# Storing batches 4 and 5 by chosen DMA engines among the loads, and batch 11 in one transfer

## The chip, the cores and the metric

The kernel runs on one core of one Trainium2 chip. Times are device microseconds of one execution; lower is better. The kernel before takes 124.91 us (median of 3 runs, 124.83 to 125.43). The 16 DMA engines of the core are called by number, as the prediction does. The trace names none of them: a number stands for the share of the transfers that I planned for an engine. "SP's queue" and "ACT's queue" are the two that the page lists as hardware_dynamic (q1 with the stores, 18.70 MB, and q10 with the loads, 31.46 MB), "GpSimd's queue" the one that it lists as software_dynamic (q0, 0.18 MB). A run over 1.5% above the fastest of its kernel counts as slow. Each ratio is against the kernel before on the same chip and in the same rounds, so kernels are compared by their ratios and not by their times.

## The reference

```python
batch, m, k, n = 16, 512, 512, 512      # a: [16,512,512], b: [16,512,512], float32
return np.matmul(a, b.transpose(0, 2, 1)).astype(np.float32)
```

32 MB come in and 16 MB go out. The result is allowed to be computed in bf16 with float32 sums.

## The kernel before

Batches are worked on in eight pairs. Sixteen loads of 2 MB (even numbers from `a`, odd from `b`) are issued far ahead on ACT's queue (load 1 on SP's) into seven input buffers. DVE casts to bf16, PE transposes and multiplies, ACT copies the result from PSUM into one of seven output buffers (the eviction), and SP issues the stores. ACT must find output buffer `n % 7` free, so batch `n` waits for the store of batch `n - 7`. And the stores of SP's queue land in the order in which they were issued (batches 4 and 6 at 84.89 and 99.82 us).

```python
def landed(n):
    return s_st[n % NO], 16 * (n // NO + 1)          # NO = 7 output buffers
...
# ACT, pair u, half e
n = 2 * u + e
if n >= NO:
    nc.scalar.wait_ge(*landed(n - NO))
for j in range(J):
    nc.scalar.wait_ge(s_mm, J * n + j + 1)
    c = nc.scalar.copy(out=ob[:, n % NO, j, :]..., in_=ps[:, j, :]...)
...
# SP: batch X = 11 in pieces, every other batch in one transfer of 8 KB rows
store(n, lo=1, hi=J - 1)...                           # its middle rows, 128 partitions
store(n, step=J - 1, part=slice(32, 96))...
for i in range(4):
    store(n, step=J - 1, part=slice(i, 16, 4))...     # four partitions, planned for engines 0 to 3
store(n, step=J - 1, part=slice(16, 20))...           # engine 4's by plan, sent as four partitions
# GpSimd: the rest of batch 11, each time behind a dummy read of five rows
for i in range(4):
    nc.gpsimd.dma_start(turn[:5, i], a[0, :5, :64]...)
    for part in (slice(20 + i, 32, 4), slice(96 + i, P, 4)):
        store(X, step=J - 1, part=part, engine=nc.gpsimd)
```

The pieces of batch 11 are meant to take 16 KB off engine 4. The dummy reads are meant to move the next transfers on by five engines.

## Time and profile before

| | before |
|---|---|
| time | 124.91 us |
| span of the profiled execution | 123.3 us |
| DMA strip | full from slice 2 to 39 of 40 |
| last load lands | 99.78 us |
| last stores issued, landed | 114.33, 122.19 us |
| ACT's waits for a store | 1.50 us (batch 11), 4.42 us (batch 13) |

A strip has 40 equal slices; a digit is the busy share in tenths. The prediction shows the strips and ACT's waits, and how they are read. PE around the second to last pair: the second half of the transposes, then the 32 matmuls of the pair (columns: start, duration, engine, line, operation, out from in, count, and the idle time ahead).

```profile
88.82 1.05 PE L223 MATMUL tp<-ident,ha 128*128 128x128 bf16 x16 [0.68 <-PEq L135]
90.02 1.05 PE L223 MATMUL tp<-ident,hb 128*128 128x128 bf16 x16
90.91 7.29 PE L242 MATMUL ps<-tb,ta 128*128 128x512 bf16 x32
```

PE idles 0.68 us and then runs (90.9 to 98.2 us). The first matmuls of the last pair and the last copies of the run are:

```profile
105.55 7.29 PE L242 MATMUL ps<-tb,ta 128*128 128x512 bf16 x32
...
112.44 1.07 ACT L201 COPY ob<-ps 128x512 f32<-128x512 f32 x2 [0.60 <-PE ps L242]
```

The end of the run in stretches of 2 us (last two columns: DMA share and GB/s):

```profile
114.00:116.00 2.00, 0.00 (x0) 0.00 (x0) 0.00 (x0) 0.00 (x0) 0.00 (x0) 1.00 0.99 418
116.00:118.00 2.00, 0.00 (x0) 0.00 (x0) 0.00 (x0) 0.00 (x0) 0.00 (x0) 1.00 1.04 441
```

All compute is done, and the DMA engines work off the stores.

### The profile page before, as it was taken

The numbers are of one execution on the slowest core, as the hardware profiler recorded it, in microseconds if no ns is written. First come the engines' busy times: TensorE is split into PE (matmuls) and PEld (weight loads), VectorE is DVE, ScalarE is ACT, GpSimd is POOL, SyncE is SP. The second block draws the span as 40 slices with busy tenths as digits, with TensorE's granted clock in tenths as the row PEclk, the third lists the DMA queues.
The fourth block names the chain that finished last, engine by engine and source line by source line (L and its number), as shares of the span: only waits on it lengthen the run. The fifth ranks groups of instructions, "written<-read, shape, count | busy, mean of one in ns | idle before, by whom it ended". The sixth has DMA issues, their size and how long they took to land. (4 is left out here: it accounts for less than half of the span.)

```text
span 123.3 us, 2255 instructions
## 1 busy us (share of the span) xinstructions
PE 90.2 (73%) x768; PEld 54.8 (44%) x768; DVE 67.9 (55%) x96; ACT 67.9 (55%) x130; POOL 8.5 (7%) x18
## 2 busy tenths in 40 slices
PE   0000089999999899989998999999799917996000
PEld 0000078447744764574477347645654506542000
DVE  0000598982896589388918974872977059400000
ACT  0400064567855966696589468765866069656000
POOL 2000000000000000000000000000000039910000
PEclk9999999999999999999999999999999999999965
DMA  4999999999999999999999999999999999999991
GB/s 112 404 425 425 441 431 431 431 431 441 425 436 425 425 361 415 444 423 425 431 433 425 431 423 425 436 444 428 423 423 441 412 423 423 432 397 432 425 407 72
DMA packets 5341, 50.35 MB, mean 408 GB/s; under 512 B 904, under 2 KB 904, under 8 KB 1500
## 3 DMA queue, kind: packets, MB, share of 16 engines
q10 hardware_dynamic: 2160, 31.46, 60.5%
q1 hardware_dynamic: 2796, 18.70, 36.2%
q0 software_dynamic: 384, 0.18, 0.5%
q14 instruction: 1, 0.01, 0.0%
HBM read 33.56 MB, written 16.78 MB: 408 GB/s over the span
## 5 line engine op out<-in xcount | busy, mean ns | idle before, releaser
L242 PE MATMUL ps<-tb,ta 128*128 128x512 bf16 x256 | 57.8, 379 | 0.4
L201 ACT COPY ob<-ps 128x512 f32<-128x512 f32 x64 | 34.2, 591 | 27.8 <-PE ps L242 21.9
L181 ACT COPY ta<-tp 128x512 bf16<-128x512 bf16 x64 | 33.0, 612 | 13.7 <-PE tp L223 13.2
L242 PEld LDWEIGHTS ps<-tb,ta 128*128 128x128 bf16 x256 | 24.1, 98 | 30.6 <-issue 4.0
L223 PE MATMUL tp<-ident,ha 128*128 128x128 bf16 x256 | 18.6, 224 | 18.7 <-PEq L135 18.2
L223 PEld LDWEIGHTS tp<-ident,ha 128*128 128x128 bf16 x256 | 15.8, 100 | 22.3 <-issue 20.5
L168 DVE COPY tb<-tp 128x1024 bf16<-128x1024 bf16 x32 | 21.2, 685 | 3.6 <-DVEq L135 3.6
L223 PE MATMUL tp<-ident,hb 128*128 128x128 bf16 x256 | 17.6, 223 | 3.5 <-PEq L135 3.3
L223 PEld LDWEIGHTS tp<-ident,hb 128*128 128x128 bf16 x256 | 15.4, 100 | 4.7 <-issue 4.4
L154 DVE CAST ha<-ld 128x1024 bf16 x8 | 5.5, 690 | 14.6 <-POOLq L108 13.8
L163 DVE COPY ha<-wa 128x2048 bf16<-128x2048 bf16 x8 | 5.5, 691 | 12.7 <-DVEq L135 12.7
L154 DVE CAST hb<-ld 128x1024 bf16 x8 | 5.5, 689 | 7.9 <-DVEq L135 7.9
L158 DVE CAST wa<-ld 128x2048 bf16 x8 | 9.8, 1220 | 0.0
L158 DVE CAST wb<-ld 128x2048 bf16 x8 | 9.8, 1220 | 0.0
L114 POOL DMA_DIRECT2D turn<-in_a_dram x4 | 2.7, 663 | 98.9 <-ACT ob L201 98.9
L155 DVE CAST ha<-ld 128x1024 bf16 x8 | 5.5, 687 | 0.0
L155 DVE CAST hb<-ld 128x1024 bf16 x8 | 5.5, 686 | 0.0
L167 DVE COPY hb<-wb 128x2048 bf16<-128x2048 bf16 x8 | 5.5, 684 | 0.0
L98 POOL DMA_DIRECT2D out_dram<-ob x8 | 5.2, 651 | 0.0
L176 ACT ACT_TABLE_LOAD x1 | 1.3, 1283 | 4.1 <-issue 4.1
L78 POOL TENSOR_SCALAR_AFFINE_SELECT ident<-ident 128x128 bf16<-128x128 bf16 x1 | 0.3, 288 | 0.2 <-POOL ident L76 0.2
L76 POOL MEMSET ident<- 128x128 bf16 x1 | 0.2, 205 | 0.5 <-SPq L41 0.5
(5 smaller groups left out, 0.6 us busy)
## 6 DMA issues: line engine op xcount, KB each, us to landing
ld<-in_a_dram ACTq DMA_DIRECT2D x8, 2048.0 KB, 29.1
ld<-in_b_dram ACTq DMA_DIRECT2D x7, 2048.0 KB, 26.8
out_dram<-ob SPq DMA_DIRECT2D x14, 1024.0 KB, 29.0
ld<-in_b_dram SPq DMA_DIRECT2D x1, 2048.0 KB, 12.5
out_dram<-ob SPq DMA_DIRECT2D x1, 768.0 KB, 8.0
out_dram<-ob SPq DMA_DIRECT2D x1, 512.0 KB, 24.5
out_dram<-ob SPq DMA_DIRECT2D x2, 256.0 KB, 7.9
out_dram<-ob POOLq DMA_DIRECT2D x4, 32.0 KB, 6.0
```

The lines of the kernel that those rows point to most:

```text
L98: return engine.dma_start(out[n].rearrange("(p j) n -> p j n", j=J)[part, rows], ob[part, n % NO, rows])
L114: nc.gpsimd.dma_start(turn[:5, i], a[0, :5, :64].rearrange("p (x k) -> p x k", x=2)[:, :, :16]).then_inc(s_y, 16)
L154: nc.vector.tensor_copy(out=h[:, :J, :], in_=src[:, :J, :HK])
L155: nc.vector.tensor_copy(out=h[:, J:, :], in_=src[:, J:, :HK]).then_inc(s_c, 1)
L158: nc.vector.tensor_copy(out=w[:], in_=src[:, :, HK:]).then_inc(s_w, 1)
L163: nc.vector.tensor_copy(out=ha[:], in_=wa[:]).then_inc(s_ca, 1)
L167: nc.vector.tensor_copy(out=hb[:], in_=wb[:]).then_inc(s_cb, 1)
L168: nc.vector.tensor_copy(out=tb[:, ko, :], in_=tp[:, 2 + ko % 2].rearrange("k j p -> k (j p)"),).then_inc(s_eb, 1)
L181: c = nc.scalar.copy(out=ta[:, ko, e * J * P:(e + 1) * J * P].rearrange("k (j p h) -> k j p h", j=J, h=2), in_=tp[:, ko % 2, :, e * HP:(e ...
L201: c = nc.scalar.copy(out=ob[:, n % NO, j, :].rearrange("m (p j) -> m p j", j=2 * J), in_=ps[:, j, :].rearrange("m (j p) -> m p j", j=2 * J),)
L223: t = nc.tensor.transpose(tp[:, 2 * x + g, j, :], h[:, j, g * P:(g + 1) * P], ident[:])
L242: t = nc.tensor.matmul(ps[:, j, :], ta[:, ko, (e * J + j) * P:(e * J + j + 1) * P], tb[:, ko, :].rearrange("k (j p) -> k j p", j=2 * J)[:, ...
```

## The change

The intent: move the piecewise stores from batch 11, near the end, to batches 4 and 5, among the loads; send full 8 KB rows; and take 32 KB off engine 4 in place of 16.

```diff
-    X = 11
+    X = 4
...
+        def store_two(part, engine):                      # both batches, 8 KB per row and batch
+            return engine.dma_start(
+                out[X:X + 2].rearrange("e (p j) n -> p e (j n)", j=J)[part],
+                ob[part, X % NO:X % NO + 2].rearrange("p e j n -> p e (j n)"))
+        def spare(i):                                      # on GpSimd's queue
+            last = [slice(96 + i, P, 4)]
+            if i < 2:
+                nc.gpsimd.dma_start(turn[:5, i], ...)      # dummy read of five rows
+                parts = [slice(20 + i, 32, 4)]
+            elif i == 2:
+                parts = [slice(16, 17), slice(17, 18), slice(16 + i, 32, 4)]
+            else:
+                parts = [slice(i, 32, 4)]
+            for part in parts + last:
+                store_two(part, nc.gpsimd).then_inc(s_y, 16)
+            # called for i = 0, 1 after load 9 and for i = 2, 3 after load 10
...
-            # SP: batch 11 in seven transfers (cut)
+            # SP
+            if n == X + 1:
+                for part in (slice(32, 96), *(slice(i, 16, 4) for i in range(3))):
+                    store_two(part, nc.sync).then_inc(s_x, 16)
...
+                if n == X + NO:                            # ACT, batch 11
+                    nc.scalar.wait_ge(s_x, 16 * 4)
+                    nc.scalar.wait_ge(s_y, 16 * 12)
-                if n >= NO:
+                elif n >= NO and n != X + 1 + NO:
                     nc.scalar.wait_ge(*landed(n - NO))
```

Batch 11 now waits for both batches 4 and 5, and batch 12 for nothing.

More of the change, by code (lines that the diff above doesn't have):

```diff
@@ L93, in landed, with store @@
         def landed(n):
-            return s_st[n % NO], 16 * (n // NO + 1)
-        def store(n, lo=0, hi=J, step=1, part=slice(0, P), engine=nc.sync):
-            rows = slice(lo, hi, step)
+            return s_st[n % NO], 16 * (n // NO + (n % NO not in (X, X + 1)))
+        def store(n, lo=0, hi=J):
+            return nc.sync.dma_start(
+                out[n].rearrange("(p j) n -> p j n", j=J)[:, lo:hi], ob[:, n % NO, lo:hi]
+            )
+        def store_two(part, engine):
             return engine.dma_start(
-                out[n].rearrange("(p j) n -> p j n", j=J)[part, rows], ob[part, n % NO, rows]
+                out[X:X + 2].rearrange("e (p j) n -> p e (j n)", j=J)[part],
+                ob[part, X % NO:X % NO + 2].rearrange("p e j n -> p e (j n)"),
             )
@@ L105 @@
             load(n, nc.scalar)
+        def spare(i):
+            last = [slice(96 + i, P, 4)]
+            if i < 2:
+                nc.gpsimd.dma_start(
+                    turn[:5, i], a[0, :5, :64].rearrange("p (x k) -> p x k", x=2)[:, :, :16]
+                ).then_inc(s_y, 16)
+                parts = [slice(20 + i, 32, 4)]
[5 more added lines that the diff above has]
+                store_two(part, nc.gpsimd).then_inc(s_y, 16)
         for n in range(2 * pairs):
             nc.gpsimd.wait_ge(s_ld[n % NL], 16 * (n // NL + 1)).then_inc(s_go, 1)
-        nc.gpsimd.wait_ge(s_out, X + 1)
-        for i in range(4):
-            nc.gpsimd.dma_start(
-                turn[:5, i], a[0, :5, :64].rearrange("p (x k) -> p x k", x=2)[:, :, :16]
-            ).then_inc(s_y, 16)
-            for part in (slice(20 + i, 32, 4), slice(96 + i, P, 4)):
-                store(X, step=J - 1, part=part, engine=nc.gpsimd).then_inc(s_y, 16)
+            if n in (X + 5, X + 6):
+                nc.gpsimd.wait_ge(s_out, X + 2)
+                for i in range(2):
+                    spare(2 * (n - X - 5) + i)
         nc.sync.wait_ge(s_ld[0], 32)
@@ L122 @@
             nc.sync.wait_ge(s_out, n + 1)
-            if n != X:
+            if n == X + 1:
+                for part in (slice(32, 96), *(slice(i, 16, 4) for i in range(3))):
+                    store_two(part, nc.sync).then_inc(s_x, 16)
+            elif n != X:
                 store(n, hi=J if n < batch - 1 else J - 1).then_inc(landed(n)[0], 16)
-                continue
-            store(n, lo=1, hi=J - 1).then_inc(landed(n)[0], 16)
-            store(n, step=J - 1, part=slice(32, 96)).then_inc(s_x, 16)
-            for i in range(4):
-                store(n, step=J - 1, part=slice(i, 16, 4)).then_inc(s_x, 16)
-            store(n, step=J - 1, part=slice(16, 20)).then_inc(s_x, 16)
         def taker(engine):
@@ L256 @@
     with tc.tile_critical(sync_engine=act, no_gpsimd_drain=True):
-        nc.scalar.wait_ge(s_x, 16 * 6)
-        nc.scalar.wait_ge(s_y, 16 * 12)
         for n in range(batch - NO, batch):
```

## The prediction

> **What bounds the kernel now.** I read the strips of busy tenths first, then the DMA queues, the chain that ended last, the waits, and last the trace's list of packets and of semaphore updates (one update per DMA engine and transfer), which shows each engine's own end.
>
> ```profile
> PE   0000089999999899989998999999799917996000
> PEclk9999999999999999999999999999999999999965
> DMA  4999999999999999999999999999999999999991
> GB/s 112 404 425 425 441 431 431 431 431 441 425 436 425 425 361 415 444 423 425 431 433 425 431 423 425 436 444 428 423 423 441 412 423 423 432 397 432 425 407 72
> ...
> HBM read 33.56 MB, written 16.78 MB: 408 GB/s over the span
> ```
>
> The 16 DMA engines are full from the second slice to the last but one, at 397 to 444 GB/s but for one slice of 361, while PE is idle for the last 10 us. The kernel is a fixed 50.35 MB pushed through a full pipe: only less work on the pipe, or a more even end of its 16 engines, can shorten it. Two phases:
>
> ```profile
> core 0: us, PE busy (x) PEld busy (x) DVE busy (x) ACT busy (x) POOL busy (x), PEclk, DMA share, GB/s
> ...
> 53.00:99.00 46.00, 43.77 (x379) 26.22 (x376) 31.51 (x45) 30.46 (x59) 0.00 (x0) 1.00 1.01 428
> ...
> 105.00:114.00 9.00, 7.78 (x45) 3.50 (x42) 1.29 (x2) 5.45 (x11) 3.39 (x7) 1.00 1.03 416
> ```
>
> Until 99.8 us loads and stores share the pipe; after that stores alone, and while GpSimd's small transfers run the rate is 416 rather than 428. The chain that ended last is useless here as a bound: it gives 5.4% of the span to PE and 0.9% to the last evictions, and ends at 113.5 us, before the last stores. What it leaves out is the queue of stores behind it: the last 256 KB are issued at 114.33 us and land at 122.19.
>
> The waits matter because the change moves one of them:
>
> ```profile
> ACT ob L201 <- PE ps L242: 21.9, 28, 1.2
> ACT ta L181 <- PE tp L223: 13.2, 4, 10.8
> ACT ob L201 <- DMA out_dram<-ob: 5.9, 2, 4.4
> ```
>
> ```profile
> 84.91 2.05 ACT L201 COPY ob<-ps 128x512 f32<-128x512 f32 x4 [1.50 <-DMA out_dram<-ob]
> ...
> 99.84 2.05 ACT L201 COPY ob<-ps 128x512 f32<-128x512 f32 x4 [4.42 <-DMA out_dram<-ob]
> ```
>
> The 1.50 is batch 11 waiting for the store of batch 4 (same output buffer of seven; landed at 84.89), the 4.42 is batch 13 waiting for batch 6 (99.82).
>
> The packet list gives unit costs: a 16 KB packet takes 611 ns of one engine, 8 KB 309, 4 KB 159, 2 KB 84. The semaphore updates give the laggard. Fifteen engines have signalled batch 10's store by 109.22 us, the sixteenth at 110.35: 1.13 us late. After batch 11, which takes 16 KB off one engine, the lag is 0.56 (batch 12: 114.27 and 114.83), and 0.58 on the very last transfer (121.61 and 122.19). In the packet list the pipe empties between 120.4 and 121.1 us, except one engine that runs alone to 121.7.
>
> [...] the spare semaphore of batch 11 has 16 + 5 x 4 updates by engines plus 5 early ones, as one 16-engine and five 4-engine transfers would give. [...] between 53 and 99 us 2 MB of loads (16 KB packets) land per 7.33 us beside 1 MB of stores (8 KB packets). [...]
>
> **The change, part by part.**
>
> 1. Engine 4's share. Of batches 4 and 5 each engine normally writes 8 partitions x 2 x 8 KB = 128 KB. [...] after the change engines 0 to 3 write 136 KB, engine 4 96 KB, the rest 128. Before, in batch 11, engine 4 gave up 4 x 4 KB = 16 KB and engines 0 to 3 took 4 KB each. Net: engine 4 does 16 KB less, two packets x 309 ns = 0.62 us; engines 0 to 3 do 4 KB more, 0.15 us. If engine 4 is the laggard, it trails by only 0.58 us, so the end moves to the second-latest engine: 122.19 - 121.61 = 0.58 us at most, 0.43 if one of engines 0 to 3 is that second one.
> 2. Batch 11's rows. Today: 128 packets of 4 KB x 159, 168 of 2 KB x 84, 44 of 4 KB by GpSimd x 159 = 41.5 us of packet time; as 128 x 309 it is 39.6. The 1.9 us over 16 engines is 0.12 us. Two of four dummy reads go too (nothing). From the fill of the window 105 to 114 (416 against 428: 0.25 us over 9 us) the gain may be up to 0.25. I take 0.15.
> 3. Timing of loads. GpSimd's share of batches 4 and 5 is 832 KB: 64 KB on each of engines 5 to 15, 32 on engine 4, 24 on 0 to 3. It is issued after loads 9 and 10 have landed (55.9 and 63.2 us) and so comes as a third queue in the mixed phase, where before there were two. The loads behind it shift by 64 KB = 8 x 309 ns = 2.4 us on engines 5 to 15. The last load, 99.78 today, lands at about 102.0. Before to after the last load the work is fixed: 99.78 to the first matmul of the last pair at 105.55 is 5.77, so that pair starts at about 107.8 and ends about 2.3 us late.
> 4. Batch 11's wait. Its buffer is now free only when batches 4 and 5 are both out. On engines 0 to 3 the SP queue must finish 4 x 64 + 112 = 368 KB, where batch 5 before was the 384th KB, out at 90.1 to 91. 16 KB less is 1.8 us less at 7.33 us per 64 KB; 24 KB from GpSimd is 0.9 more: about 89.8, with stragglers 90.5. So the 1.50 us wait that ended at 84.91 ends about 90.5, though the data is ready about 2.4 us later too. The 4.42 us wait for batch 6 goes, since that store now lands by about 97.5 and batch 13 is not ready until 101. From 90.5: four copies 2.05, then `ta` 2.1, second half of the transposes and matmuls from about 96; 7.3 of matmul, and 4.9 from there to the next pair's first matmul (as 86.02 to 90.91 today): 108.2. It ties with the loads' 107.8.
> 5. Does the later compute reach the end? The last stores are issued 2.5 us later: batch 14 at 111.38 + 2.5 = 113.9, the last at 116.8. A load issued at 0.92 had its first packet at 1.96, so data flows 1.04 us after issue: 114.9. With 2 MB left at 2.46 us per MB and the pipe empty at about 120.6, batch 14 is needed at 115.6. The slack of today (3.2 us) shrinks to 0.7, but is not used up.
>
> Sum: 0.5 (part 1) + 0.15 (part 2), parts 3 to 5 hidden: 124.91 - 0.65 = 124.26. I take 124.3.
>
> **Rivals.** (a) The late compute starves the pipe at 115 us. Against it: 0.7 us of slack; for it: each microsecond that batch 11's wait ends after 90.5 comes off that slack, and then off the end. If the wait ends at 92.5, the kernel comes to about 125.5. (b) The laggard is not engine 4 but, say, one of engines 0 to 3, which get more: then the end would be later by 0.15, some 125.0. Against it: the lag halved from 1.13 to 0.56 just across batch 11, and 16 KB is 0.6 us. (c) GpSimd's issues, 0.56 to 1.14 us each today, sit in the loop that tells DVE of landed loads; six of them take 3.5 to 6 us, less than the 7.3 between loads, and the pair they could delay waits for batch 11's buffer anyway. No effect. (d) More gain: the pipe in the store phase runs at 428 throughout; then 123.7.
>
> **Range and chances.** Gains are capped by the second-latest engine (0.58) and the packet time; losses by the starved pipe, of which I give 20%, worth up to 1 us or more. 8 in 10: 123.7 to 125.2. A change over 2% needs 2.5 us: 2% for faster, as nothing that large is on the pipe, and 4% for slower.
>
> **What would show it.** Right: the last transfer's sixteenth update within 0.2 us of the fifteenth; GpSimd's queue at 0.85 MB; the last load landing about 2 us later; one wait of `ob` for a store, ending near 90.5; DMA strip full to slice 39. Wrong: a slice below 9 near 115 us in the DMA strip, or two waits for stores; the lag unchanged at 0.6, which would mean the wrong engine was relieved.

## The result, and the profile after

The changed kernel takes 126.95 us (126.74 to 127.12, 6 runs) against 125.08 us for the kernel before in the same rounds: ratio 1.0148, 95% interval 1.0127 to 1.0168. A ratio here is the mean time of one kernel's fast runs over that of the other's of the same rounds, so it is not quite the ratio of the medians. The change loses 1.5%, clearly outside the range predicted.

The strips of the changed kernel:

```profile
PE   0000189999999899989999998998304999999900
PEclk9999999999999999999999999999955589999995
DMA  3999999999999999999999999999999999999393
GB/s 105 435 435 424 424 429 435 435 445 424 419 424 424 429 364 432 448 398 432 435 416 430 414 443 419 435 424 424 445 411 437 427 416 429 416 424 388 152 422 123
```

The third digit from the end of the DMA strip is a hole: 152 GB/s in a slice of 3.1 us. PE has a gap at slices 29 to 31, half its clock (digit 5) in slices 30 to 32, and is then busy until two slices from the end, where before it was three. The same two stretches of the end:

```profile
114.00:116.00 2.00, 2.00 (x11) 0.89 (x10) 0.00 (x0) 1.23 (x3) 0.00 (x0) 1.00 0.77 324
116.00:118.00 2.00, 2.00 (x11) 0.88 (x9) 0.00 (x0) 1.07 (x2) 0.00 (x0) 1.00 0.12 49
```

PE and ACT are still at work while the DMA engines have run dry. At 428 GB/s these two stretches lose 2 x (1 - 324/428) + 2 x (1 - 49/428) = 2.3 us of transfer. Going back from there, ACT's waits and its copies of batch 11:

```profile
ACT ob L217 <- DMA out_dram<-ob: 9.0, 1, 9.0
...
92.35 2.05 ACT L217 COPY ob<-ps 128x512 f32<-128x512 f32 x4 [9.00 <-DMA out_dram<-ob]
...
118.21 1.07 ACT L217 COPY ob<-ps 128x512 f32<-128x512 f32 x2 [0.60 <-PE ps L258]
```

There is one wait in place of two, and it ends at 92.35 us. The last copies begin at 118.21 where before they began at 112.44. And PE in the pair behind that wait:

```profile
95.53 1.99 PE L239 MATMUL tp<-ident,ha 128*128 128x128 bf16 x16 [5.53 <-PEq L148]
97.31 1.91 PE L239 MATMUL tp<-ident,hb 128*128 128x128 bf16 x16
99.02 8.12 PE L258 MATMUL ps<-tb,ta 128*128 128x512 bf16 x32
...
111.32 7.29 PE L258 MATMUL ps<-tb,ta 128*128 128x512 bf16 x32
```

After 5.53 us of idleness the transposes take 1.99 and 1.91 us where they took 1.05, and the matmuls 8.12 where they took 7.29: the granted clock was 0.50 from 90.88 to 101.12 us. The last transfer's 16 updates come between 123.89 and 124.13 us. The laggard seems gone, but this proves nothing: an engine that was behind may have caught up while the others stood idle in the hole.

### The profile page after: what moved, and what is told of

The parts are those of the page before. It is cut to its first block, busy times and chain, and to the rows that moved or that the text cites.

```text
span 125.2 us, 2250 instructions
## 1 busy us (share of the span) xinstructions
PE 92.5 (74%) x768; PEld 56.6 (45%) x768; DVE 68.2 (54%) x96; ACT 68.0 (54%) x130; POOL 8.4 (7%) x18
## 5 line engine op out<-in xcount | busy, mean ns | idle before, releaser
L258 PE MATMUL ps<-tb,ta 128*128 128x512 bf16 x256 | 58.7, 384 | 0.4
L239 PE MATMUL tp<-ident,ha 128*128 128x128 bf16 x256 | 19.6, 230 | 23.0 <-PEq L148 22.5
L239 PEld LDWEIGHTS tp<-ident,ha 128*128 128x128 bf16 x256 | 16.5, 102 | 26.9 <-issue 25.1
L239 PE MATMUL tp<-ident,hb 128*128 128x128 bf16 x256 | 18.5, 230 | 2.7 <-PEq L148 2.7
L239 PEld LDWEIGHTS tp<-ident,hb 128*128 128x128 bf16 x256 | 16.3, 103 | 3.5 <-issue 3.2
L103 POOL DMA_DIRECT2D out_dram<-ob x10 | 5.9, 595 | 3.1 <-ACT ob L217 3.1
L120 POOL DMA_DIRECT2D turn<-in_a_dram x2 | 1.9, 926 | 54.8 <-DMA ld<-in_b_dram 54.8
## 6 DMA issues: line engine op xcount, KB each, us to landing
ld<-in_b_dram SPq DMA_DIRECT2D x1, 2048.0 KB, 12.3
```

Source lines behind the costliest of these rows:

```text
L103: return engine.dma_start(out[X:X + 2].rearrange("e (p j) n -> p e (j n)", j=J)[part], ob[part, X % NO:X % NO + 2].rearrange("p e j n -> p ...
L120: nc.gpsimd.dma_start(turn[:5, i], a[0, :5, :64].rearrange("p (x k) -> p x k", x=2)[:, :, :16]).then_inc(s_y, 16)
L239: t = nc.tensor.transpose(tp[:, 2 * x + g, j, :], h[:, j, g * P:(g + 1) * P], ident[:])
L258: t = nc.tensor.matmul(ps[:, j, :], ta[:, ko, (e * J + j) * P:(e * J + j + 1) * P], tb[:, ko, :].rearrange("k (j p) -> k j p", j=2 * J)[:, ...
```

## The experiments

Thirteen kernels ran, and all gave correct results. Theory A is the late release of batch 11's buffer and what follows from it. Theory B is that GpSimd's transfers among the loads cost the time as such, C that batch 11 in one transfer does. D and E came up on the way.

**1. The wait alone.** The kernel before, with no transfer changed:

```diff
-                    nc.scalar.wait_ge(*landed(n - NO))
+                    nc.scalar.wait_ge(*landed(n - NO + (n == 11)))
```

> The kernel before, with one wait changed: batch 11's eviction waits for the store of batch 5 (lands near 92.4 us) in place of batch 4 (84.9). No transfer is changed. Theory A (the late release of batch 11's buffer and what follows of it on PE empties the store queue): the last pair's copies end near 118 to 119 us in place of 113.5, the DMA strip has a hole of 2 to 3 us near 116, time 127.3 to 127.8, ratio 1.018 to 1.022 (the hole, without the change's gain). Theory B (GpSimd's transfers among the loads and the later last load cost the time): 125.1, ratio 1.000. Theory C (batch 11 in one transfer costs it): 125.1.

Measured: 125.92 us (125.29 to 126.69), ratio 1.0090 (1.0050 to 1.0130). The wait ends at 91.51, the last copies begin at 116.90, and the strip has the hole:

```profile
DMA  4999999999999999999999999999999999999793
GB/s 122 408 423 423 434 429 423 445 434 439 434 423 429 429 352 431 439 405 431 421 426 455 421 421 434 413 439 431 429 429 431 416 421 431 412 412 424 304 416 124
```

So the wait by itself makes a loss of 0.9%, with no transfer touched, against B and C. The size was missed by half: the wait ended 0.8 us sooner than in the changed kernel, the last copies came 1.3 us sooner, and from 114 to 118 us some 0.9 us of transfer are lost (356 and 311 GB/s) against 2.3.

**2. The transfers without the wait.** An eighth output buffer was not tried. The input buffer of load 9 has been read by 62 us and is never filled again, so batches 11 and 12 can be evicted into it:

```diff
+        def obuf(n):
+            if n in (11, 12):
+                return ld[:, 2, (n - 11) * J:(n - 10) * J, :]
+            return ob[:, n % NO]
...
-                if n == X + NO:  ...wait for s_x and s_y
+                if n >= NO and n not in (11, 12):
```

> The changed kernel, with batches 11 and 12 evicted into an input buffer that is no longer used, so that nothing waits for batches 4 and 5; all transfers stay. Theory A: no wait for a store at batch 11, no hole in the DMA strip, last transfer's 16 updates within 0.25 us, time 124.2 to 124.6, ratio 0.993 to 0.996. Theory B: still 126.5 to 127, ratio 1.013, with the last load still landing near 102. Theory C: the same 127.

Measured: 125.35 us (125.21 to 125.44), ratio 1.0033 (1.0013 to 1.0054).

```profile
DMA  5999999999999999999999999999999999999991
GB/s 143 398 430 424 430 430 430 430 430 430 424 430 435 424 382 390 448 419 440 409 424 433 422 430 432 422 414 427 427 451 424 435 406 430 424 422 424 424 411 42
```

The hole is gone, and with it 1.0148 - 1.0033 = 1.15%, or 1.4 us. That is theory A. But the kernel is still slower than before, not 0.5% faster: the other half of my expectation failed. The last transfer's updates say where: eleven engines finish by 121.21 us, three at 121.4 to 121.5, one at 122.07 and one at 122.42. Something other than engine 4's old lag holds the end.

**3. The wait where it can be made up.** Batches 2 and 3 in place of 4 and 5, so that batch 9 waits:

```diff
-    X = 4
+    X = 2
```

> The changed kernel with batches 2 and 3 in place of 4 and 5, so that the buffer that comes free late is wanted by batches 9 and 10, two pairs before the end's last three. Theory A: a wait of 3 to 6 us at batch 9 that ends near 76.5 us, made up again because a pair takes 11.5 us of PE but 14.6 us of loads; no hole at 116, time 124.2 to 124.7, ratio 0.993 to 0.997. Theory B (the transfers themselves): 127.

Measured: 125.36 us (125.32 to 125.69), ratio 1.0041 (1.0019 to 1.0063), with no hole and this wait:

```profile
77.89 2.05 ACT L217 COPY ob<-ps 128x512 f32<-128x512 f32 x4 [6.09 <-DMA out_dram<-ob]
```

Again the hole is cured and the gain does not come. Its updates end as in experiment 2: two engines at 122.18 and 122.40, the rest by 121.64.

**What the packets say (theory D).** The trace lists every packet with start, duration and size but not its engine. Yet on a full engine the next packet starts 3 or 4 ns before the one before ends, so packets can be chained into 16 engines, and each engine's role read from its own sequence on GpSimd's queue (a dummy read shows 128 bytes, a row 8 KB). Checked on the kernel without any special transfer (experiment 4), the chains give every engine the 3,072 KB that it must have (one of them 8 KB more, a packet of the kind that the page lists as instruction). For experiment 2 they give:

```
engines (by their part in GpSimd's transfers)   KB in all       last packet ends, us
0, 1 (got both one-row transfers)               3104, 3112      121.74, 122.10
2, 3                                            3088            121.18, 121.19
4                                               3040            120.58
5 to 11                                         3072            120.49 to 120.95
12 to 15                                        3056            120.21 to 120.60
planned: 0 to 3 3080, 4 3040, the rest 3072
```

(One engine's 8 KB of instructions are in the 3112.) The two one-row transfers, rows 16 and 17, went to the same two engines, and what follows went four engines lower than planned. (The expectations below call the place at which GpSimd's next transfer starts the cursor.) Two engines carry 32 KB more than most, 4 x 309 ns = 1.2 us: that is the late end. Engine 4 was relieved as planned. In the kernel before, the chains confirm it as the laggard: it ends at 121.73, the rest by 121.16, although it has 16 KB less; its packets took 3.1 us longer than the standard duration of their sizes, those of the other engines 1.1 to 1.6.

**4. No chosen engines at all.** The kernel before with batch 11 as an ordinary store, and nothing on GpSimd's queue:

```diff
-            if n != X:
-                store(n, hi=J if n < batch - 1 else J - 1).then_inc(landed(n)[0], 16)
-                continue
-            # the seven transfers of batch 11, and GpSimd's twelve (cut)
+            store(n, hi=J if n < batch - 1 else J - 1).then_inc(landed(n)[0], 16)
```

> The kernel before without any transfer by chosen engines: each batch goes in one transfer (the last one in two). It says what 16 KB off one engine and the 2 KB rows of batch 11 are worth. My reading of the laggard: the last transfer's sixteenth update comes 1.1 us after the fifteenth (0.58 in before), the other engines end 0.15 us earlier; time 125.4 to 125.6, ratio 1.003 to 1.005. If the special transfers of batch 11 were a loss in themselves: below 125.0.

Measured: 125.26 us (124.94 to 125.67), ratio 1.0030 (1.0006 to 1.0055). The sixteenth update comes at 122.03, the fifteenth at 121.39: 0.64 us apart, not 1.1. The direction was right, and the other engines do end 0.2 us earlier than before (121.39 against 121.61). By the ratios, relieving engine 4 by 16 KB was worth about 0.3% (interval 0.06 to 0.55), net of the small rows that it took. The two profiles are weaker evidence, as the lag itself differs between executions: at batch 6, before any relief, the sixteenth update was 0.22 us late here and 0.87 in the kernel before.

**5. Repair of the placing, first try.** Experiment 2 with a dummy read of two rows after each one-row transfer:

```diff
             for k, part in enumerate(parts + last):
                 store_two(part, nc.gpsimd).then_inc(s_y, 16)
+                if i == 2 and k < 2:
+                    nc.gpsimd.dma_start(turn[:2, 2 + k], a[0, :2, :64]...).then_inc(s_y, 16)
```

> The kernel with freed buffers (125.35 us), plus two dummy reads of two rows on GpSimd's queue, one after each of the two one-row transfers. Chaining the packets of that run by their end times puts both one-row transfers on the same two DMA engines, and everything after them four engines too low: two engines write 32 KB more than the rest in all and end 1.2 us late, where the plan was 8 KB on each of four. Theory D (this misplacing eats the gain): the dummies put each row on its own pair; four engines have 8 KB more, the last transfer's sixteenth update falls from 122.4 to about 121.4, time 124.2 to 124.5, ratio 0.994 to 0.997. If the second row stays on the first pair in spite of the dummy: 124.5 to 124.8. Rival (GpSimd's transfers among the loads cost as such, misplaced or not): 125.3 as without the dummies.

Measured: 124.83 us (124.66 to 125.04), ratio 0.9976 (0.9957 to 0.9995), the first one below 1. The last update is at 122.00, not 121.4. The chains show the second case that I had written down: the dummies moved what follows to the right engines, but both rows still went to engines 0 and 1 (3,088 KB), with 2 and 3 at 3,072. 16 KB of excess are gone from each of two engines, and 0.57% of the time with them.

**6. Does a small packet cost a turn (theory E)?** The changed kernel, with SP's three four-row transfers each cut in two; same bytes, same engines:

```diff
-                for part in (slice(32, 96), *(slice(i, 16, 4) for i in range(3))):
-                    store_two(part, nc.sync).then_inc(s_x, 16)
+                store_two(slice(32, 96), nc.sync).then_inc(s_x, 16)
+                for i in range(3):
+                    for e in range(2):
+                        store(X + e, part=slice(i, 16, 4)).then_inc(s_x, 16)
```

> The changed kernel with each of the three four-row transfers on SP's queue cut into two, one per batch: the same bytes on the same engines, three more semaphore packets on each of engines 0 to 3. Theory E (a semaphore packet takes a turn like any packet, in which another queue's 16 KB packet of 0.61 us passes): batch 11's wait ends about 1.8 us later, near 94.2 in place of 92.35; the hole grows, time 128.3 to 129. Rival (bytes alone set when the buffer comes free): 92.4, time 126.9.

Measured: 128.42 us (127.09 to 129.29, 4 runs, the highest of them slow), ratio of the fast runs 1.0214 (1.0162 to 1.0267). The wait of batch 11:

```profile
93.89 2.05 ACT L219 COPY ob<-ps 128x512 f32<-128x512 f32 x4 [10.43 <-DMA out_dram<-ob]
```

It ends 1.54 us later with not a byte more: three semaphore packets on each of four engines cost 0.51 us each, near the 0.61 us of the load packet that passes in the meantime. The semaphore updates of the changed kernel agree: its three small transfers end on the last of engines 0 to 3 at 87.63, 89.89 and 92.33 us, 2.3 and 2.4 us apart, where two 8 KB packets take 1.83 at 7.33 us per 64 KB. In the chains a load packet stands behind each of these semaphore packets. The kernel before shows the same turns from 53 to 99 us: of 798 load packets of 16 KB, 797 are followed on their engine by a packet of SP's queue; of 808 store packets of 8 KB, 788 are followed by a packet of the loads' queue; and of 111 semaphore packets of SP's queue all are, 105 of them by one of 16 KB. The time follows the wait by the ratio, 1.0214 against 1.0148, though the two intervals touch: two fast runs took 128.33 and 128.51 us, as expected, and one 127.09.

**7. No relief of engine 4, but the rest of the change.** All of rows 0 to 31 by GpSimd in eight-row transfers, no one-row transfer, no extra transfers on SP's queue:

```diff
-                for part in (slice(32, 96), *(slice(i, 16, 4) for i in range(3))):
+                for part in (slice(32, 96),):
...
-            if i < 2:      # dummy and parts as planned
-            elif i == 2:
+            # for every i: parts = [slice(i, 32, 4)], no dummy
```

> The changed kernel without any relief of engine 4: rows 0 to 31 all go by GpSimd's queue in eight transfers of eight rows, rows 32 to 95 by SP's, no one-row transfer, no dummy read, every engine 128 KB. Theory A and D: SP's queue ends the pair near 86.5 us, so batch 11 waits 2 to 3 us and no hole opens; engine 4 is the only late one again (sixteenth update 0.6 us after the fifteenth); time 125.0 to 125.4, ratio 1.001 to 1.005. Theory B (any storing by GpSimd among the loads costs): 126 or more.

Measured: 125.48 us (125.19 to 125.86), ratio 1.0039 (1.0018 to 1.0059). There is no hole, the sixteenth update is 0.87 us after the fifteenth, and the wait is short:

```profile
86.53 2.05 ACT L217 COPY ob<-ps 128x512 f32<-128x512 f32 x4 [3.42 <-DMA out_dram<-ob]
```

Without the extra transfers on SP's queue (48 KB and three semaphore packets on each of engines 0 to 3) the buffer comes free 5.8 us sooner. GpSimd's storing among the loads costs nothing by itself that these runs resolve (0.39% with full lag, where experiment 4 without it has 0.30%), against B once more.

**8. Control.** The kernel before with the freed input buffer of experiment 2 (its `obuf`, and no wait at 11 and 12).

> Control: the kernel before with batches 11 and 12 evicted into the same unused input buffer. The kernel before never starves the store queue, so freeing its 1.5 us wait gives nothing: 124.9, ratio 0.998 to 1.002. If the freed buffers themselves gained or lost, the runs with them would have to be read against this one.

Measured: 124.88 us (124.72 to 125.29), ratio 0.9985 (0.9963 to 1.0006): nothing resolved, as expected. So 0.9976 in experiment 5 may not be read as a gain of the placing alone; over this control it is 0.1%, which these runs do not resolve.

**9 to 11. A repair that was none.** Rows 16 and 17 as two transfers of two rows, one per batch:

```diff
-                parts = [slice(16, 17), slice(17, 18), slice(16 + i, 32, 4)]
+                for e in range(2):
+                    nc.gpsimd.dma_start(out[X + e]...[16:18], ob[16:18, (X + e) % NO]...).then_inc(s_y, 16)
+                parts = [slice(16 + i, 32, 4)]
```

Once on top of experiment 2, once on the changed kernel, once on experiment 3:

> The kernel with freed buffers, with rows 16 and 17 sent by GpSimd as two transfers of two rows (one per batch) in place of two of one row. The run with the dummy reads showed that the one-row transfers both land on the same pair of engines wherever the cursor stands, while two-row transfers move it. Theory D: now four engines write 8 KB more and engine 4 32 KB less, as planned; the last transfer's sixteenth update comes near 121.4 us, no engine more than 0.4 us late; time 124.3 to 124.6, ratio 0.993 to 0.997, the best so far. If the misplaced rows were not what held the end: as with freed buffers alone, 1.003.

> The changed kernel with that one repair alone; batch 11 still waits for batches 4 and 5. GpSimd's share on the two worst engines falls from 48 to 24 KB, so by theory A and D batch 11's wait ends about 0.9 us sooner, near 91.4 in place of 92.35, the hole is shorter but stays: time 125.8 to 126.4, ratio 1.006 to 1.011. If placing did not matter for the wait: 92.3 us and 1.015.

> The same repair with batches 2 and 3 as the pair and no freed buffers: the wait falls on batch 9 (about 5 us, ending near 77), and is made up. Theory A and D together say that this needs no more memory and gives the same as freed buffers: last update near 121.4, time 124.3 to 124.7, ratio 0.993 to 0.998. If a wait of 5 us and PE's lower clock cost something wherever they fall: 1.005 or more.

Measured: 125.29 us, ratio 1.0016 (1.0003 to 1.0029); 126.54 us (125.73 to 127.69, the highest of six runs slow), ratio 1.0112 (1.0076 to 1.0147); 125.37 us, ratio 1.0019 (1.0006 to 1.0032). All three missed what was expected of the repair, for one reason: the chains show the same misplacing as in experiment 2. So the middle one is no test of the placing. Its wait ends at 92.37 and its strip has the hole again. The first and third give the size of the misplacing a range: four kernels with it and without a hole stand at 1.0016 to 1.0041.

The third run shows by chance what PE's clock does. It is experiment 3 over again, with the same wait (6.02 against 6.09 us) and nearly the same idleness of PE ahead (4.64 and 4.71 us). In experiment 3 the matmuls behind it took

```profile
84.57 8.20 PE L258 MATMUL ps<-tb,ta 128*128 128x512 bf16 x32
```

and here

```profile
84.65 7.18 PE L263 MATMUL ps<-tb,ta 128*128 128x512 bf16 x32
```

because the granted clock was back at 1.00 sooner: 0.50 in the stretch 84 to 86 us of experiment 3 and 0.79 from 86 to 88, 0.79 and 1.00 here. What a stall of PE costs beyond itself thus differed by 1.0 us between two profiles of the same stall.

**12 and 13. A repair that places the rows.** Two transfers of two rows x two batches x half a row, as in the chains so far only copies with a third dimension (listed in the trace as [2,3] to [2,8]) had moved the place of the next; on top of experiment 2 and of experiment 3:

```diff
+                for h in range(2):
+                    cols = slice(h * J * N // 2, (h + 1) * J * N // 2)
+                    nc.gpsimd.dma_start(out[X:X + 2]...[16:18, :, cols],
+                                        ob[16:18, X % NO:X % NO + 2]...[:, :, cols]).then_inc(s_y, 16)
+                parts = [slice(16 + i, 32, 4)]
```

> Two-row transfers of plain 8 KB rows turned out to be placed like the one-row ones: both on the first pair of engines, the cursor not moved (packet chains of that run: 48 KB of GpSimd's data on two engines, 32 on two, as before the repair). The transfers that do follow the cursor all have a third dimension. So here rows 16 and 17 go in two transfers of two rows x two batches x half a row. Theory D: the second one lands on the next pair; four engines have 8 KB more and engine 4 32 KB less; last update at 121.4 to 121.8, time ratio 0.993 to 0.998, at or below the run with dummy reads (0.9976). If the placing is not what held the end: 1.002 to 1.004 again.

> The same with batches 2 and 3 as the pair and no freed buffers. Theory A and D together: the wait at batch 9 (5 to 6 us) is made up, nothing else differs from the run with freed buffers; last update at 121.4 to 121.8, ratio 0.993 to 0.998. If the wait costs wherever it falls: above 1.002.

Measured on experiment 2: 124.70 us (124.48 to 125.31), ratio 0.9978 (0.9955 to 1.0001). Four engines now have 24 KB of GpSimd's data and engine 4 has 32, as planned, and the last update is at 122.02. The 16 updates lie within 0.24 us, which fits a short hole: ACT waited 4.06 us for transposes of the last pair where it waited 3.01 in experiment 2, the last copies began at 116.10, 1.2 us later than in experiment 2, and the stores seem to have run just dry (393 GB/s from 116 to 118 us). Measured on experiment 3: 125.22 us (124.61 to 125.69), ratio 1.0009 (0.9983 to 1.0036). In its profiled run the wait at batch 9 lasted 7.57 us and ended 1.7 us later than in experiment 3, the copies at the end were 1.5 us later, and the hole was back:

```profile
GB/s 116 402 434 423 434 434 429 445 429 423 429 429 423 429 405 408 410 421 432 414 434 435 408 437 429 424 447 410 434 434 431 437 408 423 421 421 431 302 413 116
```

It was GpSimd's queue that ended this wait: its last transfer landed at 79.51, SP's at 76.75, and the two repaired transfers took 5.1 us of it (63.37 to 68.49), where the one-row ones of experiment 3 took 3.2. So my claim that a wait two batches earlier is always made up does not hold: waits of 6.02 and 6.09 us were made up, one of 7.57 was not. The best kernel by ratio is that of experiment 5; 12 equals it within the intervals.

In one table (wait of the batch concerned: when it ended in the profiled run):

| experiment | ratio | wait ends, us | hole | placing |
|---|---|---|---|---|
| changed kernel | 1.0148 | 92.35 | 2.3 us | missed |
| 1 wait alone | 1.0090 | 91.51 | 0.9 us | as before |
| 2 freed buffers | 1.0033 | none | no | missed |
| 3 batches 2 and 3 | 1.0041 | 77.89 | no | missed |
| 4 no chosen engines | 1.0030 | 83.82 | no | none |
| 5 freed, dummies | 0.9976 | none | no | half repaired |
| 6 six transfers | 1.0214 | 93.89 | yes | missed |
| 7 no relief | 1.0039 | 86.53 | no | even |
| 8 before, freed | 0.9985 | none | no | as before |
| 9 freed, two-row transfers | 1.0016 | none | no | missed |
| 10 changed, two-row transfers | 1.0112 | 92.37 | yes | missed |
| 11 batches 2 and 3, two-row transfers | 1.0019 | 77.98 | no | missed |
| 12 freed, repaired | 0.9978 | none | short | as planned |
| 13 batches 2 and 3, repaired | 1.0009 | 79.58 | yes | as planned |

## Why the prediction was wrong

By its own parts:

1. *Engine 4 is the laggard, and relieving it pays.* That it is the laggard is right: the chains of packets show it in the kernel before, where the engine with 16 KB less ends at 121.73 us and the rest by 121.16. That another 16 KB off it pays is not shown: over the control, experiments 5 and 12 gain 0.1%, which these runs do not resolve. Wrong in the placing: "engines 0 to 3 write 136 KB" rested on my assumption that each transfer on GpSimd's queue goes on to the engines behind those of the one before. The two one-row transfers do not: the chains of experiment 2 show both rows on engines 0 and 1, and what follows four engines lower than planned. Why they are placed so was not shown. This term was -0.5 us in my sum. Experiments 2 and 5 differ by 0.57%, 0.7 us, for 16 KB of the misplaced excess; against all four misplaced kernels without a hole it is 0.4 to 0.65%.
2. *Batch 11's rows, 0.15 us.* Not separated by a run. The fifteenth update of experiment 4, 0.22 us earlier than before, agrees with it, but engines 0 to 3 write 4 KB less there too.
3. *The last load at about 102.0.* Right: 101.96.
4. *Batch 11's wait ends about 90.5.* This step failed: 92.35. I counted bytes, and left out that each of the three extra transfers on SP's queue brings a semaphore packet, which takes a turn. Experiment 6 measured 1.54 us for three of them, against the 1.85 missing. The misplaced rows are a second cause: they put 24 KB more than planned on engines 0 and 1. With the rows in place (experiment 12) the last of SP's extra transfers landed at 91.84, against 92.34 in experiment 2, so they are worth about 0.5 us. The store of batch 6 landed at 99.64, not 97.5; that cost nothing, as batch 13 came later still.
5. *The later compute does not reach the end.* This step failed, and with it the forecast: the overlap that was to hide parts 3 and 4 was not there. The last copies were 5.8 us later than before, not 2.5, which used up the slack of 3.2 us and opened a hole of 2.3 us. Of the 3.3 us that I had missed, 1.85 are the later wait of part 4. Another 1.2 lie between the end of the wait and the pair's first matmul: I had taken 5.5 us, the kernel before takes 6.0 (84.91 to 90.91), and here it was 6.7 (92.35 to 99.02), as PE came out of its idleness at a granted clock of 0.50. The matmuls behind it took 8.12 in place of 7.29 us, but to the last pair's first matmul it was 12.3 us (99.02 to 111.32), where I had 12.2. The trace has the granted clock at 0.50 from 90.88 us, 0.88 us into the 5.53 us of idleness, to 101.12, 5.6 us after PE was back at work; in the kernel before, with 2.63 us of idleness from 99.09, it stayed at 1.00.

The sum: 1.0148 less 1.0033 is the hole, 1.4 us; it takes 2.3 us of transfer and costs less, which would fit late engines catching up in it; no run separates that. 1.0033 less 0.9976 is part of the misplaced rows, 0.7 us; 0.9976 is -0.3 us, where I had said -0.65. Of this last gap of 0.35 us, 16 KB still too much on two engines may explain some; the rest stays open, as the control with its own 0.9985 shows that 0.2% cannot be told apart in these runs.

Of the rivals, (a) was the one that happened. I gave it 20% and "some 125.5 if the wait ends at 92.5": the wait ended there, but the kernel took 126.95, as the estimate had neither the longer path behind the wait nor the misplaced rows. (b) happened in another form: not engine 4's relief but the load put on engines 0 and 1 set the end. (c) was right: no cast waited for GpSimd's issues. The one that came late (DVE, load 11, at 71.52 in place of 70.86) followed its load, which landed at 71.17 in place of 70.51.

## What to carry to other kernels

Before moving stores to an earlier place, look who waits for their buffer: here a full DMA pipe lost 1.4 us by one late buffer, where the whole change was to give 0.65. When counting what is ahead in a queue, count packets with their turns, semaphore packets included, and not bytes: here three semaphore packets cost 1.54 us. And prove from the trace, engine by engine, that a transfer lands on the DMA engine that it was meant for, as here two one-row transfers off their place moved what came behind them by four engines, and two engines got 32 KB more than most.

## What the traces show of the DMA engines

- Which engines a GpSimd copy used: copies of one or two rows of 8 KB (listed in the trace as [1,2] and [2,1]) went to engines 0 and 1 and did not move the place of the next, while those listed as [2,2], [2,3], [2,4], [2,5] and [2,8] started there and moved it. Two engines got 32 KB more than most for it, 24 KB of it not planned.
- Turns between queues: a semaphore packet of 4 bytes took a full turn. Three of them delayed a queue by 1.54 us beside 16 KB packets (experiment 6). On GpSimd's queue every transfer of the changed kernel brings 16 semaphore updates; its twelve transfers, issued by 66.8 us, landed one after the other about 2.4 us apart, the last at 88.9.
- The slow engine: the chains name engine 4, and with nothing on GpSimd's queue there was still one slow engine (0.64 us behind at the end). In the kernel before and in experiment 4 its packets took 1 to 2 us longer in all than those of the others. What slows it stays open.
